# A streaming encoder step on one core: 32-row products of the mixer grouped, three costs of its schedule set anew, last sums of squares moved in between the products

## The chip, the cores and the metric

The kernel runs on one core of one Trainium2 chip. The time is the device time of one execution in microseconds (us). Before the change three runs took 2301.47, 2303.37 and 2303.8 us; the median is 2303.37 us. One more execution was recorded by the hardware profiler; it took 2301.52 us, and from its first to its last instruction 2299.8 us.

The engines are called by short names in the profile: PE is TensorE's products, PEld its weight loads, DVE is VectorE, ACT ScalarE, POOL GpSimd, SP the queue that starts DMAs. One float32 product of the program stands in the trace as two records with a weight load each; one product of split operands stands as one record.

## The reference, cut to what matters

A batch of 544 rows (512 of a prompt, 32 of a running sample) of width 1024 passes two layers. The first has a Mamba-2 mixer, the second attention; each has two feed-forward blocks and a gated input embedding, and a final norm ends the step. The two places that the change touches are the mixer's scan and the end.

```python
def ssd_scan(xdt, a, Bm, Cm, s0, chunk_len):
    ...
        y_diag = jnp.einsum('bijg,bijge,bjgep->bigep', cb, decay, x_c)      # inside a chunk: 32 heads in 4 groups of 8
        y_off = jnp.einsum('bign,bgepn->bigep', C_c, state) * jnp.exp(a_cs)[..., None]
        ...
        return new_state, y_diag + y_off
...
        gate = jax.nn.sigmoid(rms_norm(x, ple_norm[i]) @ ple_w_gate[i])
        x = x + gate * (p[i] @ ple_w_proj[i])
    return rms_norm(x, final_norm), ...
```

The prompt is scanned in four chunks of 128 rows, the sample is a fifth chunk of 32 rows with its own carried state. The final norm needs, for each row, the sum of squares over all 1024 values of x.

## The kernel before, in words

Activations lie transposed: eight tiles `x[c]` of 128 features by 544 rows, the rows in two halves of 272. Dense weights are split into a high and a low part (`whi`, `wlo`), and a 128-by-128 block of a dense product is three matmuls for each half of 272 columns (`product`, line 284).

**The mixer** (`mamba`, line 972) runs as generators under a planner (`Plan`, line 65). Each step of a generator names an engine and a cost in us ("T" is TensorE); `Plan.run` (line 139) keeps a modelled time for each engine, always takes the step that could begin first, and writes its instructions. The engines execute in just the order so written (`ordered`), so the costs decide the order of instructions and nothing else. The dense products (`dense`, ranked last) come in the order `MSEQ = "i0 z0 i1 i2 z1 o0 i3 z2 o1 z3 o2 o3"`: inputs, gates and outputs of the four groups. Between them the planner puts the scan. For group g and chunk c, `turn_x` and `turn_b` transpose, `decay` makes `ex` (inside the chunk) and `ab` (decay times C, a POOL product), `state` makes the next `st`, and `output` (line 1318) makes y: for each of the eight heads one product with `ex` and, from chunk 1 on, one with the old state. `emit(t)` (line 1336) writes two heads h = 2t and 2t+1: head by head, first the product of `xd` and `ex` (as many rows as the chunk has), then that of `st` and `ab` (128 rows). The even head goes to partitions 0 to 63 of the result, the odd head to 64 to 127. Four such steps are written per chunk (line 1343); the planner is told 0.44 us each for chunk 0, 0.87 for chunks 1 to 3, 1.2 for the sample. In the sample chunk the first product has 32 rows and the second 128, both move 32 columns.

**The end** (`ple`, line 944, called for layer 1 at line 2050) is not under the planner: its engines' order is made by the compiler's own list scheduling. It goes through `order` (line 1995): features m = 0 to 3 with both halves, 4 to 7 with the first half, then 7, 6, 5, 4 with the second. For each, `product` into a bank `pg`, then on DVE `ft` (times the norm), on ACT a sigmoid, on DVE `fu` and the new `x`, and then `last` (line 2022), which squares x (`sq`, in the second half `sq1`), scales x on POOL, and hands the squares on. The sums of squares are TensorE products with a matrix of ones: `add_square` (line 1997) for the second half, one tile at a time, and `finish(0)` (line 2004) for the first half, both called by `last`. `finish(a)` then makes the inverse root (`ry`, `rm`, `rfin`), the outputs `out` and their DMAs. In the order of the code, `finish(0)` stands straight after the products of (7, second half), and an `add_square` after those of (6), (5) and (4); `finish(1)` writes the last one.

All instructions written through the wrapper at line 192 show as L193 in the profile; the tile names tell them apart.

Of the kernel before, what the change touches and what calls it, by code (L numbers as in the profile page):

```python
# [10 lines left out]
P = 128  # L11
D = 1024
KC = D // P
TP = 512
TS = 32
T = TP + TS
# [28 lines left out]
NZB, NY, NYH = 1, 2, 4  # L45

RGNORM, RSCAN, RCONV, RGATE, ROUT, RSTEP = 39, 4, 20, 45, 2, 41

FIRST = [0, 1, 2, 3], [0, 1, 2, 3], [0, 1, 2, 3], [0, 1, 2, 3]
GROUPS = [(4, 5), (6, 7)], [(8, 9), (10, 11)], [(12, 13), (14, 15)], [(16, 17), (18, 19), (20, 21)]  # L50
# [130 lines left out]
def _body(tc, io):  # L181
# [17 lines left out]
    V, S, G, TE = (Engine(n, e) for n, e in (("V", nc.vector), ("S", nc.scalar), ("G", nc.gpsimd), ("T", nc.tensor)))  # L199
# [4 lines left out]
    with ExitStack() as ctx:  # L204
# [66 lines left out]
        def weight_parts(pool=pool):  # L271
            return [pool.tile([P, 1024], F32R, tag=t, name=t, bufs=2) for t in ("whi", "wlo")]
# [668 lines left out]
            split(ph, pl, pr)  # L941
            return [(ph[:, k, :], pl[:, k, :]) for k in range(2)]

        def ple(i, norm, after, psum, tmp, ring, order, keep=lambda m: None):
            ps_in = ple_inputs(i, tmp)
            prj = tmp.tile([P, KC, T], F32, tag="plp", name="plp")
            for m in range(KC):
                if m % 4 == 0:
                    wp = load_w(io["wple"][i, m // 4], 1024)
                pp = psum()  # L950
                product(pp, wp, ps_in, off=(m % 4) * 256)
                S.activation(halves(prj[:, m, :]), pp[:, :, :H], AF.Copy)
            r, held = None, {}
            for m, which in order:
                def cut(v):
                    return v[:, which[0] * H:(which[-1] + 1) * H].rearrange("p (a b) -> p a b", a=len(which))
                if m not in held:
                    held[m] = load_w(io["wpg"][i, m], 1024, parts=keep(m))
                pg = psum()
                product(pg, held[m], norm.parts, which=which)  # L960
                if r is None:
                    r = norm.scale(psum, ring)
                t = tmp.tile([P, T], F32, tag="ft", name="ft", bufs=2)
                V.tensor_tensor(out=cut(t), in0=pg[:, which[0]:which[-1] + 1, :H], in1=cut(r), op=ALU.mult)
                S.activation(cut(t), cut(t), AF.Sigmoid)
                u = tmp.tile([P, T], F32, tag="fu", name="fu", bufs=2)
                V.tensor_tensor(out=cut(u), in0=cut(t), in1=cut(prj[:, m, :]), op=ALU.mult)
                V.tensor_tensor(out=cut(x[m]), in0=cut(x[m]), in1=cut(u), op=ALU.add)
                after(m, which, t)


        def mamba(norm, after, ready, ahead):
            with tc.tile_pool(name="mt", bufs=1, reuse_waits="tile") as tmp, \
# [16 lines left out]
                got = {}  # L990
# [327 lines left out]
                def output(g, c):  # L1318
                    off, n = chunks[c]
                    src = off if c < 4 else SOFF  # L1320
                    xs = got["x", g]
                    need = [("ex", g, c), ("xd", g, c), ("xw", g, c), ("cd", g, c)]
                    yield "wait", *need
                    if c > 0:
                        yield "wait", ("st", g, before(c))
                    if c == 0:
                        yield "get", "y"
                        got["y", g] = tmp.tile([P, 4, T], F32, tag="y", name="y", bufs=NY)
                        yield "set", ("y0", g)
                    else:  # L1330
                        yield "wait", ("y0", g)
                    yield "get", "aux"
                    py = aux()
                    xd, ex, ab = got["xd", g, c], got["ex", g, c], got["ab", g, c]

                    def emit(t):
                        for b in range(2):
                            h = 2 * t + b
                            dst = py[64 * b:64 * b + 64, t * P:t * P + n]
                            TE.matmul(dst, xd[:n, h, :], ex[:n, h, :], start=True, stop=c == 0)  # L1340
                            if c > 0:
                                TE.matmul(dst, got["st", g, before(c)][:, h, :], ab[:, h, :], start=False, stop=True)
                    for t in range(4):
                        yield "T", (1.2 if n < P else 0.87) if c else 0.44, lambda: emit(t)
                    yield "set", ("y", g, c)
                    yield "put", "ex"
                    yield "put", "xd"
                    yield "put", "ab"
                    pyv = py[:, :].rearrange("p (t i) -> p t i", t=4)[:, :, :n]
                    yv = got["y", g][:, :, off:off + n]  # L1350

                    def skip(t):
                        V.scalar_tensor_tensor(out=yv[:, t], in0=xs[:, t, src:src + n], scalar=dskip[:, 4 * g + t:4 * g + t + 1], in1=pyv[:, t],
                                               op0=ALU.mult, op1=ALU.add)
                    for t in range(4):
                        yield "W", v_cost(n) + 0.06, lambda: skip(t)
                    yield "put", "aux"
                    yield "set", ("out", g, c)
# [638 lines left out]
        def add_square(last=False):  # L1997

            if not total:
                total.append(psum())  # L2000
                TE.matmul(total[0][:, 1, :H], ones, acc[:, H:], start=True, stop=False, skip_group_check=True)
            TE.matmul(total[0][:, 1, :H], ones, waiting.pop(0), start=False, stop=last, skip_group_check=True)

        def finish(a):
            cols = slice(a * H, a * H + H)
            if a:
                add_square(last=True)
                at_once(rsqrt_ops(total[0], [], D, "rfin", (a,), rfin))
            else:
                at_once(rsqrt_ops(psum(), [acc, squares[a]], D, "rfin", (a,), rfin))  # L2010
            for c in range(0, KC, 2):
                o = end.tile([P, 2, H], F32, tag="out", name="out", bufs=4)
                for b in range(2):
                    if (c + b, a) in scaled:
                        e = G if a == 0 or c + b in (1, 3) else V
                        e.tensor_tensor(out=o[:, b, :], in0=x[c + b][:, cols], in1=rfin[:, cols], op=ALU.mult)
                    else:
                        V.scalar_tensor_tensor(out=o[:, b, :], in0=x[c + b][:, cols], scalar=gains[:, NORMS["fin"], c + b:c + b + 1],
                                               in1=rfin[:, cols], op0=ALU.mult, op1=ALU.mult)
                nc.sync.dma_start(io["y"][:, c:c + 2, cols], o)  # L2020

        def last(c, which, t):
            cols = slice(which[0] * H, (which[-1] + 1) * H)
            ending = (c, which) in ((7, (0,)), (4, (1,)))
            if which == (1,):
                sq = end.tile([P, H], F32, tag="sq1", name="sq1", bufs=4)
                if waiting:
                    add_square()
                waiting.append(sq)
                if ending:  # L2030
                    V.tensor_tensor(out=sq, in0=x[c][:, cols], in1=x[c][:, cols], op=ALU.mult)
                    S.activation(table, t[:, H:H + 1], AF.Abs_reciprocal_sqrt)
                else:
                    S.activation(sq, x[c][:, cols], AF.Square)
                    G.tensor_scalar(x[c][:, cols], x[c][:, cols], gains[:, NORMS["fin"], c:c + 1], 0.0, op0=ALU.mult, op1=ALU.add)
                    scaled.add((c, 1))
                if c == 7:
                    finish(0)
                return
            sq = acc if c == 0 else pool.tile([P, T], F32, tag="sq", name="sq", bufs=2)  # L2040
            if ending:
                V.tensor_tensor(out=sq[:, cols], in0=x[c][:, cols], in1=x[c][:, cols], op=ALU.mult)
                squares[0] = sq
            else:
                S.activation(sq[:, cols], x[c][:, cols], AF.Square)
                if c:
                    G.tensor_tensor(out=acc[:, cols], in0=acc[:, cols], in1=sq[:, cols], op=ALU.add)
                G.tensor_scalar(x[c][:, cols], x[c][:, cols], gains[:, NORMS["fin"], c:c + 1], 0.0, op0=ALU.mult, op1=ALU.add)
                scaled.update((c, a) for a in which)
        ple(1, np1, last, psum, tmp, few, order, lambda m: weight_parts(end) if m in (4, 5) else None)  # L2050
        finish(1)
        xg["st"].close()
        later["st"].close()
# [78 lines left out]
```

## Time and profile before

| | us |
|---|---|
| median of three runs | 2303.37 |
| profiled execution | 2301.52 |
| its span, first to last instruction | 2299.8 |
| PE busy in the span | 2267.0 (99%) |
| DVE / ACT / POOL busy | 1680.0 / 1011.1 / 575.7 |
| mixer with its approaches, 384 to 830 us: PE busy of 446 | 441.83 |
| last 38 us, 2262 to 2300: PE busy | 24.75 |

A busy time of PE is modelled from pipelined matmuls, so a busy PE is not yet one at its peak; how many records of one shape go through in a stretch says more. A row of the timeline gives the start, the length from the first record's start to the last one's end, and the number of records; the distance between two rows' starts is what a group of records costs. "granted" clock is the share of TensorE's 2.4 GHz that the chip allowed in a stretch: 1.00 is 2.4 GHz and 0.50 is 1.2 GHz.

### The profile page before, as it was taken

Reading aid. Unit: us, or ns where it says so; the run is one execution under the profiler, and the core shown is the slowest. Engines: PE = TensorE matmul, PEld = TensorE weight load, DVE = VectorE, ACT = ScalarE, POOL = GpSimd, SP = SyncE. Lnnn points to the kernel's source line nnn. Section 1 sums busy time; section 2 is a strip of 40 time slices with the busy share of each in tenths; the row PEclk is TensorE's granted clock in tenths of the full one; section 3 lists DMA queues with packets and bytes.
Section 4 is the critical chain, followed back from the end, with each engine's and each line's share of the span. In section 5 each row is a group of like instructions: output and inputs, shape, how many; then the busy total and the mean of one; then the engine's idle time right before and its main releaser. Section 6 shows DMA issues by size and latency. Waiting matters only on the chain.

```text
span 2299.8 us, 42811 instructions
## 1 busy us (share of the span) xinstructions
PE 2267.0 (99%) x17937; PEld 2207.0 (96%) x17937; DVE 1680.0 (73%) x2201; ACT 1011.1 (44%) x1489; POOL 575.7 (25%) x541
## 2 busy tenths in 40 slices
PE   9999999999999999999999999999998999999997
PEld 9999999989899999999999999999985899999997
DVE  7777786679777676777757767778678576777857
ACT  5333334567646353333345533333468353333343
POOL 1221122244324122121221122121234122221224
PEclk9999999999999999999999999999999999999999
DMA  5233323333433232333232423332311132333232
GB/s 170 85 91 106 97 67 90 112 100 94 110 97 99 75 119 79 106 93 106 65 99 91 130 81 104 100 98 65 89 45 56 47 117 86 92 106 97 67 100 76
DMA packets 111537, 213.19 MB, mean 93 GB/s; under 512 B 12400, under 2 KB 33520, under 8 KB 111344
## 3 DMA queue, kind: packets, MB, share of 16 engines
q1 hardware_dynamic: 108464, 204.92, 29.7%
q10 hardware_dynamic: 2880, 5.53, 0.7%
q8 instruction: 141, 2.31, 0.4%
q14 instruction: 52, 0.43, 0.1%
HBM read 204.83 MB, written 5.60 MB: 91 GB/s over the span
## 4 chain that ended last, share of the span: by engine, by line
PE 92%; DVE 4%; ACT 2%; issue 1%; POOL 1%; DMA 1%; SPq 0%; DVEq 0%; ACTq 0%; POOLq 0%
PE mm L193 82%; PE z L193 3%; PE aux L193 3%; PE o L193 1%; PE f L193 1%; PE tr L193 1%; DVE wlo L193 1%; ACT whi L193 1%; DVE xl L193 1%; POOL ab L193 0%; DVE x L193 0%; DVE e L193 0%; DMA wraw<-in_wpg 0%; DVE fu L193 0%; DVE rm L193 0%
## 5 line engine op out<-in xcount | busy, mean ns | idle before, releaser
L193 PE MATMUL mm<-xh,whi 128*128 128x272 f32 x2096 | 513.0, 293 | 2.3 <-DVE x L193 1.0
L193 PE MATMUL mm<-xh,wlo 128*128 128x272 f32 x2096 | 506.2, 289 | 1.8 <-DVE wlo L193 1.8
L193 PE MATMUL mm<-xl,whi 128*128 128x272 f32 x2096 | 507.7, 290 | 0.3 <-DVE xl L193 0.3
L193 PEld LDWEIGHTS mm<-xh,whi 128*128 128x128 f32 x2096 | 358.6, 189 | 10.5 <-issue 7.2
L193 PEld LDWEIGHTS mm<-xh,wlo 128*128 128x128 f32 x2096 | 358.3, 189 | 2.3 <-DVE wlo L193 2.2
L193 PEld LDWEIGHTS mm<-xl,whi 128*128 128x128 f32 x2096 | 358.3, 190 | 0.7 <-DVE xl L193 0.7
L193 ACT ACTIVATE whi<-wraw 128x1024 fp32r<-128x1024 f32 (+3 forms) x215 | 184.2, 858 | 374.5 <-PE mm L193 263.3
L193 PE MATMUL mm<-xfh,whi 128*128 128x272 f32 x1152 | 332.4, 289 | 0.0
L193 PE MATMUL mm<-xfl,whi 128*128 128x272 f32 x1152 | 332.3, 288 | 0.0
L193 PE MATMUL mm<-xfh,wlo 128*128 128x272 f32 x1152 | 332.2, 288 | 0.0
L193 DVE TENSOR_TENSOR wlo<-wraw,whi 128x1024 fp32r<-128x1024 f32 (+3 forms) x252 | 257.0, 1020 | 72.6 <-ACT whi L193 54.6
L193 PE MATMUL mm<-hh,whi 128*128 128x272 f32 x1408 | 291.5, 288 | 0.0
L193 PE MATMUL mm<-hh,wlo 128*128 128x272 f32 x1408 | 291.1, 288 | 0.0
L193 PE MATMUL mm<-hl,whi 128*128 128x272 f32 x1408 | 290.9, 288 | 0.0
L193 ACT ACTIVATE whi<-a 128x1024 fp32r<-128x1024 f32 x127 | 134.9, 1062 | 319.8 <-PE mm L193 214.4
L193 DVE TENSOR_TENSOR wlo<-a,whi 128x1024 fp32r<-128x1024 f32 x145 | 178.4, 1230 | 101.7 <-ACT whi L193 67.2
L193 PEld LDWEIGHTS mm<-hl,whi 128*128 128x128 f32 x1408 | 221.5, 189 | 0.0
L193 PEld LDWEIGHTS mm<-hh,whi 128*128 128x128 f32 x1408 | 221.2, 188 | 0.0
L193 PEld LDWEIGHTS mm<-hh,wlo 128*128 128x128 f32 x1408 | 220.7, 189 | 0.0
L193 PEld LDWEIGHTS mm<-xfh,wlo 128*128 128x128 f32 x1152 | 217.1, 188 | 0.0
L193 PEld LDWEIGHTS mm<-xfl,whi 128*128 128x128 f32 x1152 | 217.1, 188 | 0.0
L193 PEld LDWEIGHTS mm<-xfh,whi 128*128 128x128 f32 x1152 | 217.1, 188 | 0.0
(290 smaller groups left out, 4108.0 us busy)
## 6 DMA issues: line engine op xcount, KB each, us to landing
a<-in_wgu SPq DMA_DIRECT2D x145, 512.0 KB, 3.9
wraw<-in_wd SPq DMA_DIRECT2D x128, 256.0 KB, 2.7
wraw<-in_win SPq DMA_DIRECT2D x41, 512.0 KB, 3.6
wraw<-in_wgu SPq DMA_DIRECT2D x29, 512.0 KB, 3.7
wraw<-in_wd SPq DMA_DIRECT2D x32, 384.0 KB, 3.1
ab<-acs_d SPq DMA_DIRECT2D x16, 512.0 KB, 4.7
wraw<-in_wout SPq DMA_DIRECT2D x16, 512.0 KB, 3.6
wraw<-in_wpg SPq DMA_DIRECT2D x16, 512.0 KB, 3.6
```

What stands on the lines that cost most here:

```text
L193: ins = getattr(self.engine, op)(*args, **kw)
```

## The change

It has three parts. In the mixer, the sample chunk's sixteen products are written as one step: first all eight with 32 rows, then all eight with 128 rows, the even and odd head still in turn; the planner is told 1.8 us for all. For the other chunks the cost of a step is 0.24 (chunk 0) and 0.46 (chunks 1 to 3). In the end, `ple` writes its product feature block by feature block and calls `between` after four of the eight; through it, `finish(0)` comes amid the products of (6, second half), and one `add_square` each amid those of (5) and (4); `finish(1)` writes the last two. In layer 0 `ple` gets no `between`, and its instructions stay the same.

```diff
+TSSD = 0.24, 0.46
...
-                product(pg, held[m], norm.parts, which=which)
+                for c in range(KC):
+                    if c == KC // 2 and between:
+                        between(m, which)
+                    product(pg, held[m], norm.parts, only=c, which=which)
...
-                    for t in range(4):
-                        yield "T", (1.2 if n < P else 0.87) if c else 0.44, lambda: emit(t)
+                    def emit_sample():
+
+                        for old in range(2):
+                            for h in range(8):
+                                t, b = divmod(h, 2)
+                                dst = py[64 * b:64 * b + 64, t * P:t * P + n]
+                                if old:
+                                    TE.matmul(dst, got["st", g, before(c)][:, h, :], ab[:, h, :], start=False, stop=True, skip_group_check=True)
+                                else:
+                                    TE.matmul(dst, xd[:n, h, :], ex[:n, h, :], start=t == 0, stop=False, skip_group_check=True)
+                    if n < P:
+                        yield "T", 1.8, emit_sample
+                    else:
+                        for t in range(4):
+                            yield "T", TSSD[c > 0], lambda: emit(t)
...
             if a:
+                add_square()
                 add_square(last=True)
...
-                if waiting:
-                    add_square()
...
-                if c == 7:
-                    finish(0)
...
+        def between(m, which):
+
+            if which == (1,) and m == 6:
+                finish(0)
+            elif which == (1,) and m < 6:
+                add_square()
```

## Rows read from the trace of the kernel before

**Rows 1.** The page: busy time and share of the span (part 1), and the chain of work that ended last, by engine (part 4).

```profile
PE 2267.0 (99%) x17937; PEld 2207.0 (96%) x17937; DVE 1680.0 (73%) x2201; ACT 1011.1 (44%) x1489; POOL 575.7 (25%) x541
...
PE 92%; DVE 4%; ACT 2%; issue 1%; POOL 1%; DMA 1%; SPq 0%; DVEq 0%; ACTq 0%; POOLq 0%
```

**Rows 2.** Who PE waited for between 384 and 830 us (the mixer with its approaches): us in total, times, longest.

```profile
PE aux L193 <- POOL ab L193: 1.2, 2, 0.9
PE aux L193 <- POOL xw L193: 0.9, 1, 0.9
PE aux L193 <- DVE btok L193: 0.8, 1, 0.8
PE mm L193 <- DVE wlo L193: 0.7, 1, 0.7
```

**Rows 3.** The timeline of PE around the sample chunk of groups 0, 1, 2 and 3: start, us from the first record's start to the last one's end, operation, shape, records. The sample's products are `aux<-ex,xd` (32 rows) and `aux<-ab,st` (128 rows); the last row of each stretch is the work after them.

```profile
487.78 0.30 PE L193 MATMUL aux<-ex,xd 32*64 32x32 f32 x2
488.94 0.30 PE L193 MATMUL aux<-ab,st 128*64 128x32 f32 x2 [0.86 <-POOL ab L193]
...
492.38 0.82 PE L193 MATMUL mm<-xh,whi 128*128 128x272 f32 x2
...
580.17 0.30 PE L193 MATMUL aux<-ex,xd 32*64 32x32 f32 x2
580.40 0.30 PE L193 MATMUL aux<-ab,st 128*64 128x32 f32 x2
...
583.84 1.40 PE L193 MATMUL aux<-xw,btok 128*128 128x512 f32 x2
...
633.44 0.30 PE L193 MATMUL aux<-ex,xd 32*64 32x32 f32 x2
...
637.10 0.52 PE L193 MATMUL mm<-yh,whi 128*128 128x272 f32 x2
...
741.26 0.30 PE L193 MATMUL aux<-ex,xd 32*64 32x32 f32 x2
741.85 0.30 PE L193 MATMUL aux<-ab,st 128*64 128x32 f32 x2 [0.29 <-POOL ab L193]
...
745.44 0.82 PE L193 MATMUL mm<-xh,whi 128*128 128x272 f32 x2
```

**Rows 4.** PE's groups by shape between 430 and 826 us: busy us, mean ns of one record.

```profile
L193 PE MATMUL aux<-ex,xd 32*64 32x32 f32 x64 | 9.5, 228 | 0.0
```

**Rows 5.** The timeline of PE where products of 64 weight columns stand in a run: a chunk of 128 rows with both kinds of product (482 us), chunk 0 of group 2, which has the products with `ex` alone (588 us), and, in the attention, four records of 32 rows ahead of records of 128 rows (1766 us).

```profile
482.08 0.45 PE L193 MATMUL aux<-ex,xd 128*64 128x128 f32 x4
482.35 0.40 PE L193 MATMUL aux<-ab,st 128*64 128x128 f32 x4
482.57 0.44 PE L193 MATMUL aux<-ex,xd 128*64 128x128 f32 x4
...
588.55 1.09 PE L193 MATMUL aux<-ex,xd 128*64 128x128 f32 x16
589.58 0.49 PE L193 MATMUL aux<-C,B 128*128 128x128 f32 x2
...
1766.03 0.43 PE L193 MATMUL o<-an,vt 32*64 32x128 f32 x4
1766.39 0.33 PE L193 MATMUL o<-sa,vc 128*64 128x128 f32 x2
```

**Rows 6.** Stretches of 3.4 us that follow the sample chunks of groups 0, 1, 2 and 3: us, PE busy (records), granted clock, DMA share, GB/s.

```profile
492.40:495.80 3.40, 3.40 (x16) 0.50 0.59 159
...
584.56:587.97 3.41, 3.41 (x15) 0.50 0.58 154
...
637.10:640.50 3.40, 3.40 (x29) 1.00 0.51 153
...
745.00:748.40 3.40, 3.40 (x17) 0.50 0.21 77
```

**Rows 7.** A stretch of the scan of group 1: us, then busy time (and instructions) of PE, PEld, DVE, ACT and POOL, granted clock, DMA share, GB/s.

```profile
520.00:555.00 35.00, 35.00 (x280) 33.70 (x279) 31.40 (x57) 24.56 (x43) 13.40 (x20) 1.00 0.29 93
```

**Rows 8.** The timeline of PE in the last 30 us: the sums of squares (products with ones).

```profile
2273.57 0.62 PE L193 MATMUL mm<-acc,ones 128*128 128x272 f32 x2
2274.95 0.73 PE L193 MATMUL mm<-sq,ones 128*128 128x272 f32 x2 [0.77 <-DVE sq L193]
...
2283.58 0.73 PE L193 MATMUL mm<-sq,ones 128*128 128x272 f32 x2 [0.97 <-ACT sq L193]
...
2287.15 0.62 PE L193 MATMUL mm<-sq,ones 128*128 128x272 f32 x2
2289.79 0.73 PE L193 MATMUL mm<-sq,ones 128*128 128x272 f32 x2 [2.02 <-DVE sq L193]
```

**Rows 9.** The timelines of DVE, ACT and POOL in the same stretch.

```profile
2274.46 0.44 DVE L193 TENSOR_TENSOR sq<-x 128x272 f32<-128x272 f32 x1
...
2281.43 0.71 DVE L193 TENSOR_TENSOR fu<-ft,plp 128x272 f32<-128x272 f32 x1 [0.95 <-ACT ft L193]
...
2288.34 0.44 DVE L193 TENSOR_TENSOR fu<-ft,plp 128x272 f32<-128x272 f32 x1 [0.56 <-ACT ft L193]
...
2279.67 1.28 ACT L193 ACT_TABLE_LOAD   x1 [1.78 <-DVE ft L193]
...
2286.25 0.95 POOL L193 TENSOR_SCALAR x<-x,gains 128x272 f32<-128x272 f32 x2
```

More of the change, by code (lines that the diff above doesn't have):

```diff
@@ L942, in ple_inputs, with ple @@
             return [(ph[:, k, :], pl[:, k, :]) for k in range(2)]
-        def ple(i, norm, after, psum, tmp, ring, order, keep=lambda m: None):
+        def ple(i, norm, after, psum, tmp, ring, order, keep=lambda m: None, between=None):
             ps_in = ple_inputs(i, tmp)
@@ L2049, in last @@
                 scaled.update((c, a) for a in which)
-        ple(1, np1, last, psum, tmp, few, order, lambda m: weight_parts(end) if m in (4, 5) else None)
+        def between(m, which):
[3 more added lines that the diff above has]
+                add_square()
+        ple(1, np1, last, psum, tmp, few, order, lambda m: weight_parts(end) if m in (4, 5) else None, between)
         finish(1)
```

## The prediction

> **What bounds the kernel now.** I read the page first: PE is busy for 99% of the span and takes 92% of the chain that ended last [rows 1]. So a change is worth what it takes from PE's own queue, or from the places where PE stands still. A busy PE need not do much, though, so in the mixer I looked at the waits and then at single stretches of the timeline. Between 384 and 830 us PE stands still for only 446 - 441.83 = 4.2 us, and the largest entries are waits of 0.7 to 1.2 us for single products of POOL and DVE [rows 2]. The mixer is bound by the order and the pace of PE's records, and nothing else hides what is saved there. DVE comes next: 31.4 of 35 us in the densest stretch of the scan [rows 7], which leaves it below PE everywhere.
>
> The reader should see three things. First, the sample chunk, the smallest of five, takes PE longest. Its sixteen products last 4.60, 3.67, 3.66 and 4.18 us in groups 0 to 3 (from the first row to the work after them [rows 3]), 16.1 us together; a chunk of 128 rows does the same sixteen, with four times the columns, at 0.22 us for four records [rows 5], so 32 records in 1.76 us. Second, right after three of these four blocks the granted clock is 0.50 for 3.4 us, that is 1.2 instead of 2.4 GHz, and 15 to 17 records go through instead of 29 [rows 6]. Third, in the last 30 us PE waits 0.77 us for a square from DVE and 0.97 us for one from ACT [rows 8].
>
> **The sample's products.** Two records of a pair span 0.30 us and one lasts about 0.22 to 0.23 [rows 3, 4], so the second starts some 0.08 after the first. The next pair starts 0.23 after the first, 0.15 after the second. That 0.15 is paid at each change between 32 and 128 rows; where 128 rows follow 128 rows it isn't seen, though heads alternate there as well [rows 5]. The attention has the same: four records of 32 rows span 0.43 at about 0.27 each, so the last starts at 0.16, and the first of 128 rows comes at 0.36, 0.20 later [rows 5]. Those four records also show that two halves of 64 output columns run side by side, at 32 rows too: four starts fit in 0.16.
>
> New block, if the halves run side by side: in each run of eight products a half has four products of two records, eight records at 0.08, so the last starts at 0.56, and 0.15 passes until the next kind: 0.71 a run, 1.42 for two. Four blocks take 5.7 us instead of 16.1, which saves 10.4. In group 0 the `ab` product of POOL is there only at 488.94 [rows 3]; the first run would be over at 487.78 + 0.71 = 488.49, so 0.45 remains a wait. In group 3 it is there at 741.85, before 741.26 + 0.71. Net **10.0 us**.
>
> The new shape, 32 rows in a run of sixteen records, isn't in the trace, so bounds: with the pace of 16 records in 1.03 us that chunk 0 has at four times the columns [rows 5], 32 records and two changes take 2.06 + 0.30 = 2.4 us, which saves 6.6. With one half after the other, 32 records at 0.08 and two changes take 2.7 us or a little more, which saves 5.3. Better than 1.42 by at most 0.3 a block (1.2 in all), if a record's start could come sooner than 0.08 after the last on its half. I take 1.42, since the row nearest in shape, the sample's own pair, has the 0.08, and the row nearest in rows has the halves side by side.
>
> The Trainium skill has a rule that speaks against the grouping: "TensorE: Matmul & The Clock Gate", the mechanism in its part on packing small matmuls, says that a weight load overlaps with running matmuls only where its row group differs. By it the old order would be the overlapped one. The row shows the contrary: 0.15 at each change of rows, 0.08 without. "TensorEngine Tiling (Array Packing)", key properties, has a change of tiling mode drain the engine, and there the trace agrees.
>
> **The clock.** Each fall costs the 29 - 16 = 13 records that didn't pass, 3.40 x 13/29 = 1.5 us. PE came out of 3.6 us of 32-column records in all three cases; group 2's block, just as long, was followed by full clock [rows 6], so it isn't certain even then. A block of 1.4 us is less than half as long; I take it that none falls: 3 x 1.5 = **4.6 us**. Bounds: 0 and 4.6.
>
> **The order.** The model's TensorE time in one group's outputs falls from 4 x 0.44 + 12 x 0.87 + 4 x 1.2 = 17.0 to 4 x 0.24 + 12 x 0.46 + 1.8 = 8.3 us, 35 us in four groups. The engine measured 0.26 (16 records in 1.03 us, four steps) and 0.44 (eight records at 0.22 per four) [rows 5], so these are near the truth and the old ones near twice it. It adds no instruction. The planner has room for more dense products between two steps of the scan, so scan products stand later in PE's queue relative to dense ones, and their inputs are the more likely there; in return POOL's and DVE's work, which the model prices as before, is packed denser against PE's time. A wrong place costs all queued behind it on PE, dense products included: the waits known from before are 0.8 to 0.9 us [rows 2]. Bounds: -2 (those for `xw`, `btok` and the rest vanish) and +18 (each of 20 chunks waits 0.9). I take **+0.5**: the old order was twice wrong in its cost and still left 4.2 us of waiting in 446.
>
> **The end.** PE's records are the same, so the gain is in the two waits. `finish(0)` now follows 12 products of (6) at 0.125 (29 in 3.4 us is 0.117, so 1.4 to 1.5 us): it comes at 2273.57 + 1.5 = 2275.1, and DVE's square is done at 2274.46 + 0.44 = 2274.90 [rows 8, 9]. The wait of 0.77 is gone. What is late next is the sum of (6)'s square, which before came 0.97 after PE was free. The chain to it (`ft`, table load, sigmoid, `fu`, `x`, square) starts when (6) is done, 0.77 earlier, but the root's table load waits for sums that are about 0.6 later; so I put the square at 2282.5 to 2282.9, and PE asks for it amid (4), at about 2283.0. Both waits go: 1.74. Against that, the last `fu` and `x` run while POOL still scales (until 2287.2), and `fu` beside POOL took 0.71 instead of 0.44 [rows 9]: 0.4 lost on the path that ends the kernel. Net **1.3 us**. Bounds: 1.74, and -1.3 if the compiler's list scheduling puts one more table load (1.28 [rows 9]) on that path. The outputs' DMAs come as before, eight on SP, four of them up to half a us later, behind nothing but themselves; the last four come 1.3 earlier. In layer 0 the split product is the same sequence, at nothing.
>
> **Sum.** 10.0 + 4.6 - 0.5 + 1.3 = 15.4 us; 2301.5 - 15.4 = 2286.1, on the profiled execution, which is 1.9 below the median of the three runs. One more fall of the clock (1.5 us) would explain most of that distance, and such a fall would go as well, so I predict **2287**.
>
> **Rivals.**
> (a) The halves don't run side by side at 32 columns, or runs of equal rows lose an overlap of weight loads: 2.7 us a block, 5.3 saved instead of 10.0, 2291. For it: the sample's records have shown no second half running yet. Against it: the attention's four records. The rule of "TensorE: Matmul & The Clock Gate" named above comes to this time too.
> (b) The new order costs 5 to 13 us of waits on PE (each of 20 chunks waiting 0.25 to 0.65 us for `ab`, `ex` or `xw`): 2291 to 2299. For it: DVE at 90% in a stretch of the scan [rows 7]; against it: the old order's small waits.
> (c) Slower: the same mechanism further on. In the new order PE stands before `aux<-ab,st` until POOL has written `ab`, in each chunk of all four groups. From 0.77 us per chunk (15.4/20) the gain is gone, and at 1.0, a little over the longest wait there is now [rows 2], the kernel takes 2301.5 + 4.6 = 2306.
> (d) The clock still falls after the blocks, as a low pace is left in them: 2291.
> (e) The change doesn't do what it says: the 0.23 per product belongs to 32 columns and not to the change of rows, the blocks stay as long and the clock falls as before; only the end gains: 2300 to 2302.
>
> **Chances.** Forecast 0.60 (2282 to 2291 by its own bounds), a 0.10, b 0.13, c 0.05, d 0.06, e 0.06. About 0.2% (4.6 us) is what a measurement of this kernel can tell from no change. Against the median, faster is below 2298.8: the forecast, a, d and most of b, 0.87; the same is e and the end of b, 0.08; slower is c, 0.05. The range from 2281 to 2296 leaves out c, e and the upper part of b, and a little at the lower end.
>
> **What would show it.** Sample blocks of 1.4 to 1.8 us with two groups of rows, 32 rows first; granted clock 1.00 between 440 and 830 us; no more than about 5 us of waits on PE in the mixer; no wait before the sums at the end, and the last sum at about 2288 less what the mixer gave, 1.3 earlier against the products. Blocks of 2.7 us speak for a, many waits for `ab` or `ex` for b or c, clock falls in spite of short blocks for d. I am wrong if PE's idle time in the mixer grows by over 5 us or if the blocks stay above 3 us.

## The result and the profile after

| | before | after |
|---|---|---|
| median, us | 2303.59 (2301.47 to 2306.64, 4 runs) | 2287.18 (2283.51 to 2288.59, 4 runs) |
| profiled execution, us | 2301.52 | 2283.51 |
| its span, us | 2299.8 | 2281.8 |

The ratio is 0.9917, interval 0.9905 to 0.9929: 16.4 us between the medians, 18.0 between the two profiled executions. The forecast was 2287. One run of an experiment below (`e2_costs`) took 3133.44 us at a mean granted clock of 0.652 and is left out of its ratio.

The page, parts 1 and 4, as [rows 1]:

```profile
PE 2252.0 (99%) x17937; PEld 2195.6 (96%) x17937; DVE 1676.6 (73%) x2201; ACT 1014.1 (44%) x1491; POOL 567.7 (25%) x540
...
PE 93%; DVE 4%; ACT 2%; issue 1%; DMA 1%; POOL 0%; DVEq 0%; SPq 0%; ACTq 0%; POOLq 0%
```

The same 17937 matmuls, PE at 99% as before: 15.0 us of busy time are gone although no record is. A page alone would not show why; the timeline of PE at the four sample chunks does (last row of each stretch: the work after them, as in [rows 3]):

```profile
500.46 0.65 PE L195 MATMUL aux<-ex,xd 32*64 32x32 f32 x16
501.05 0.66 PE L195 MATMUL aux<-ab,st 128*64 128x32 f32 x16
501.64 0.52 PE L195 MATMUL mm<-xh,whi 128*128 128x272 f32 x2
...
576.85 0.65 PE L195 MATMUL aux<-ex,xd 32*64 32x32 f32 x16
...
578.02 0.52 PE L195 MATMUL mm<-xh,whi 128*128 128x272 f32 x2
...
635.16 0.65 PE L195 MATMUL aux<-ex,xd 32*64 32x32 f32 x16
...
636.33 0.52 PE L195 MATMUL mm<-xh,whi 128*128 128x272 f32 x2
...
728.83 0.65 PE L195 MATMUL aux<-ex,xd 32*64 32x32 f32 x16
...
730.00 0.51 PE L195 MATMUL mm<-xh,whi 128*128 128x272 f32 x2
```

Each block takes 1.17 to 1.18 us; together 4.7 instead of 16.1, so 11.4 us. The stretches that follow them in groups 0, 1 and 3, where the clock fell before, as [rows 6], and the one stretch at a granted clock of 0.50 between the kernel's first and last 10 us, in the attention (us, PE busy with records, granted clock, DMA share, GB/s):

```profile
501.64:505.04 3.40, 3.40 (x31) 1.00 0.56 174
578.02:581.42 3.40, 3.40 (x32) 1.00 0.49 144
...
730.00:733.40 3.40, 3.40 (x31) 1.00 0.46 84
...
1726.96:1733.79 6.83, 6.83 (x31) 0.50 0.00 0
```

31 or 32 records at 2.4 GHz where 15 to 17 went through at 1.2 GHz: none of the three falls in the mixer is left. Who PE waited for between 384 and 825 us, as [rows 2]:

```profile
PE mm L195 <- DVE yl L195: 1.1, 1, 1.1
PE mm L195 <- DVE wlo L195: 0.7, 1, 0.7
PE mm L195 <- DVE cu L195: 0.3, 1, 0.3
```

2.1 us instead of 4.1, and other waits than before: scan products wait for nothing now, and the two new entries stand before dense products. The 0.7 for `wlo` is in both and belongs to the product behind the mixer (at 809.33, before at 826.09). The last product of the mixer's outputs (`mm<-yh,wlo`) starts at 802.44 instead of 819.20, 16.8 us earlier, although the same records ahead of the mixer stand 0.2 later (386.22 instead of 386.03); the mixer itself gained 17.0. Of that 11.4 are the blocks, 4.6 three falls of the clock at the forecast's 1.5, and 1.0 is left for the order; the waits outside the sample blocks fell by 0.8 (4.1 less the 1.2 for `ab` inside the blocks is 2.9, now 2.1).

The rest is the end. The sums of squares on PE, as [rows 8]:

```profile
2258.12 0.62 PE L195 MATMUL mm<-acc,ones 128*128 128x272 f32 x2
...
2269.33 0.73 PE L195 MATMUL mm<-sq,ones 128*128 128x272 f32 x2 [1.25 <-ACT sq L195]
...
2271.80 0.72 PE L195 MATMUL mm<-sq,ones 128*128 128x272 f32 x2 [1.75 <-DVE sq L195]
```

The waits of 0.77 and 0.97 are gone and the sums between the rows shown wait for nothing, but the sum for feature 5 now waits 1.25, where before it waited for nothing (2287.15 in [rows 8]). From the end of the products of feature 7, second half, to the last sum it was 2289.79 - 2273.57 = 16.2 us; now the first sum stands behind 12 products of feature 6 (1.5 us), so it is 2271.80 - 2258.12 + 1.5 = 15.2. The end gained 1.0 us. What is late now shows on DVE and POOL:

```profile
2264.09 6.06 POOL L195 TENSOR_TENSOR out<-x,rfin 128x272 f32<-128x272 f32 x7 [3.20 <-DVE rfin L195]
...
2265.21 1.01 DVE L195 SCALAR_TENSOR_TENSOR out<-x,gains,rfin 128x272 f32<-128x272 f32 x1
...
2267.92 0.88 DVE L195 TENSOR_TENSOR x<-x,fu 128x272 f32<-128x272 f32 x1
2268.73 0.43 DVE L195 TENSOR_TENSOR ft<-mm,r 128x272 f32<-128x272 f32 x1
...
2269.72 0.73 DVE L195 TENSOR_TENSOR fu<-ft,plp 128x272 f32<-128x272 f32 x1 [0.56 <-ACT ft L195]
...
2270.48 0.61 DVE L195 TENSOR_TENSOR x<-x,fu 128x272 f32<-128x272 f32 x1
...
2271.13 0.62 DVE L195 TENSOR_TENSOR sq<-x 128x272 f32<-128x272 f32 x1
```

PE was through with feature 4 at 2269.33 - 1.25 = 2268.08, but DVE took up its `ft` only at 2268.73, behind `x` of feature 5; and `fu`, `x` and the square take 0.73, 0.61 and 0.62. In the kernel before, the same chain (PE's last product for feature 4, then DVE; `fu` and a square of 0.44 are in [rows 9]):

```profile
2287.02 0.29 PE L193 MATMUL mm<-nh,wlo 128*128 128x272 f32 x1
2287.35 0.44 DVE L193 TENSOR_TENSOR ft<-mm,r 128x272 f32<-128x272 f32 x1 [1.71 <-PE mm L193]
...
2288.82 0.44 DVE L193 TENSOR_TENSOR x<-x,fu 128x272 f32<-128x272 f32 x1
```

There `ft` started 0.04 after PE (2287.02 + 0.29 = 2287.31), and each step of the chain took 0.44.

### The profile page after: what moved, and what is told of

Its sections match the earlier page's. It is cut to its first block, busy times and chain, and to the rows that moved or that the text cites. A ratio compares the mean times of both kernels' runs of the same rounds, so it can differ in the third digit from the quotient of the medians.

```text
span 2281.8 us, 42795 instructions
## 1 busy us (share of the span) xinstructions
PE 2252.0 (99%) x17937; PEld 2195.6 (96%) x17937; DVE 1676.6 (73%) x2201; ACT 1014.1 (44%) x1491; POOL 567.7 (25%) x540
## 4 chain that ended last, share of the span: by engine, by line
PE 93%; DVE 4%; ACT 2%; issue 1%; DMA 1%; POOL 0%; DVEq 0%; SPq 0%; ACTq 0%; POOLq 0%
PE mm L195 83%; PE z L195 3%; PE aux L195 3%; PE o L195 1%; PE f L195 1%; PE tr L195 1%; DVE wlo L195 1%; ACT whi L195 1%; DVE xl L195 1%; DVE x L195 1%; DVE e L195 0%; DVE fu L195 0%; DMA wraw<-in_wpg 0%; DMA x<-in_x 0%; DVE rm L195 0%
```

## The experiments

The theory after this result: the time in the sample blocks is paid per change between 32 and 128 rows; the clock fell because of the long, slow blocks; the two new durations matter because they put scan products behind the dense work that their inputs need; and DVE's queue took over the end. Rivals: the columns' halves, and not the changes of rows, set the blocks' pace; the clock or the order gained by chance of position; the wait at the end came from the mixer's new order or from POOL's work.

| kernel | median, us | ratio to before, interval | gain of the mixer, us |
|---|---|---|---|
| grouping alone (`e1_group`) | 2292.61 | 0.9947, 0.9932 to 0.9962 | 10.2 |
| durations alone (`e2_costs`) | 2301.95 | 0.9982, 0.9973 to 0.9991 | 1.4 |
| end alone (`e3_end`) | 2307.77, one run | | -5.3 |
| even heads first (`e4_halves`) | 2283.99, one run | | 15.3 |
| pairs of heads (`e5_pairs`) | 2285.30, one run | | 14.5 |
| feature 7 scaled by POOL (`e6_pool7`) | 2283.18 | 0.9907, 0.9894 to 0.9920 | 17.0 |
| two old durations (`e7_oldt`) | 2289.12 | 0.9940, 0.9924 to 0.9955 | 12.9 |
| the changed kernel again (`after_again`) | 2288.46 | 0.9923, 0.9911 to 0.9936 | 17.0 |

The kernel before had a median of 2306.43 us beside e1, e2, e4 and e5, and 2305.14 beside the others. The last column is from the one profiled execution of each: how much sooner than in the kernel before the last `mm<-yh,wlo` comes, counted from the record that starts there at 386.03 us. What comes ahead of the mixer is not in it; falls of the clock inside the mixer are.

**Grouping alone.** In the kernel before, with `emit_sample` as in the change, the old durations and the old end:

```diff
-                    for t in range(4):
-                        yield "T", (1.2 if n < P else 0.87) if c else 0.44, lambda: emit(t)
...
+                    if n < P:
+                        yield "T", 4.8, emit_sample
+                    else:
+                        for t in range(4):
+                            yield "T", 0.87 if c else 0.44, lambda: emit(t)
```

> The kernel before with the sample's sixteen products grouped by rows and nothing else: the planner still counts 4.8 us for them and the old costs for the other chunks, the end is as before. Theory 1 (the time went with the changes between 32 and 128 rows and with the clock falls behind them): blocks of 1.2 us in groups 1 to 3 and some 1.8 in group 0, where the product of ab is late; no granted clock of 0.50 between 440 and 830 us; 10.8 + 4.6 = 15 us less than the kernel before, 2288 to 2289. Theory 2 (the gain came from the new order of the mixer's instructions): blocks short as well, but waits take their place, and the time is above 2297.

0.9947, which is 12.2 us of 2303.6, between what the two theories had said. Three blocks are as short as in the changed kernel or nearly so (487.83 to 489.59 with a wait of 0.52 for `ab`, 630.15 to 631.32, 735.45 to 736.64); the fourth is followed by a wait of 0.43 for `xw` (575.86 to 577.53). But a new wait has come, and right after it the clock falls (timeline of PE, then the stretch with its granted clock):

```profile
583.40 1.18 PE L193 MATMUL aux<-ex,xd 128*64 128x128 f32 x16 [2.70 <-DVE y L193]
```

```profile
584.28:587.69 3.41, 3.30 (x10) 0.50 0.54 159
```

PE's waits between 384 and 825 us are 6.6 us in all, against 4.1 before and 2.1 in the changed kernel, and the mixer ends 6.6 us later than there (809.07 against 802.44); 1.5 of that is the fall of the clock. The grouping alone made PE too early for the order that the old durations had written.

**Durations alone.** The kernel before with alternating products, told at 1.8 for the sample and 0.24 and 0.46 for the rest:

```diff
-                    for t in range(4):
-                        yield "T", (1.2 if n < P else 0.87) if c else 0.44, lambda: emit(t)
+                    def emit_sample():
+
+                        for t in range(4):
+                            emit(t)
+                    if n < P:
+                        yield "T", 1.8, emit_sample
+                    else:
+                        for t in range(4):
+                            yield "T", (0.24, 0.46)[c > 0], lambda: emit(t)
```

> The kernel before with the three new costs of the schedule and nothing else: the sample's sixteen products alternate between 32 and 128 rows as before, in one step of 1.8 us, and the end is as before. Theory 1: blocks of 3.7 us, granted clock of 0.50 behind most of them, some 1 us fewer waits in the mixer: 2300 to 2304, no difference that can be measured. Theory 2: most of the gain is here, 2290 to 2294.

0.9982, 4.1 us, at the edge of what can be told from none. The waits of PE between 384 and 825 us fall to 1.0 us (0.3 for `cu` beside the row below); the 0.7 for `wlo`, at 826.45 here, lies outside, so against the 4.1 before it is 1.7. Three blocks stay at 3.67 us (502.02 to 505.69 in group 0); that of group 1 takes 4.23 (582.41 to 586.64), as the clock falls within it. The clock falls behind or within three of them, one fall of double length (PE's waits between 384 and 825 us, then the stretches with their granted clock):

```profile
PE mm L193 <- DVE yl L193: 0.7, 1, 0.7
```

```profile
506.50:509.91 3.41, 3.41 (x17) 0.50 0.56 154
585.01:591.84 6.83, 6.83 (x33) 0.50 0.53 156
649.86:653.27 3.41, 3.41 (x17) 0.50 0.52 154
```

That is one stretch of 3.4 us more than before, and one more comes at 8.15 us, ahead of the mixer. The records ahead of the mixer stand 1.75 us later than in the kernel before, and the mixer ends only 0.35 later, in spite of the 1.5 that the one stretch more inside it costs: at equal clock the order gave some 2.9 us, of which the waits explain 2.4 (4.1 to 1.7). The order has no cost of its own. The clock falls at long blocks in another order, too, though not at the same ones (groups 0, 1 and 2 here, 0, 1 and 3 before): it goes with the blocks and not with their places.

**Even heads first.** In the changed kernel, which keeps the two changes of rows:

```diff
-                            for h in range(8):
+                            for h in (0, 2, 4, 6, 1, 3, 5, 7):
```

> The changed kernel, but in each run of rows first the four even heads and then the four odd ones, so that the two halves of 64 output columns no longer take turns. The instructions and the order of all else are the same. If the short block needs both halves side by side: records at 0.058 us one after the other, 16 x 0.058 + 0.15 = 1.1 a run, 2.2 us a block, 1.0 more in each of four, and perhaps granted clock of 0.50 behind some. If turns between halves don't matter: 1.2 us a block as in the changed kernel.

The block of group 0 in its timeline of PE:

```profile
499.87 0.91 PE L195 MATMUL aux<-ex,xd 32*64 32x32 f32 x16
500.71 0.91 PE L195 MATMUL aux<-ab,st 128*64 128x32 f32 x16
501.55 0.52 PE L195 MATMUL mm<-xh,whi 128*128 128x272 f32 x2
```

A run takes 0.84 us instead of 0.59. Strictly one half after the other would be 1.03: a run is 0.44 for the eight records of a half and 0.15 for the change, so 2 x 0.44 + 0.15. Taken one by one, the starts form two rows, each with 0.058 between records; the second begins 6 ns after the fifth of the eight records of the first. So the other half does not wait until the first is through. This leaves a part of the rival: halves in turn are worth 0.5 us of a block, of 2.5 that the block lost; the changes of rows are the larger part. Over the whole mixer 1.6 us are lost against the changed kernel: 4 x 0.5, less 0.4 by which a wait for `yl` is shorter.

**Pairs of heads.** In the changed kernel, two heads with `ex`, the same two with `ab`, and so on: eight runs instead of two.

```diff
-                        for old in range(2):
-                            for h in range(8):
+                        for h0 in range(0, 8, 2):
+                            for old in range(2):
+                                for h in (h0, h0 + 1):
...
```

> The changed kernel, but the sample's products go by pairs of heads: two with 32 rows, two with 128 rows, four times; 7 changes of rows within a block instead of 1 (15 in the kernel before). If each change costs 0.15 us: two records per half at 0.08, then 0.15, 0.23 for each of eight pairs, 1.8 us a block, 0.65 more than the changed kernel in each of four groups, no clock falls. If the number of records and not the changes sets the length: 1.2 us.

The same block here:

```profile
500.49 0.30 PE L195 MATMUL aux<-ex,xd 32*64 32x32 f32 x4
500.72 0.31 PE L195 MATMUL aux<-ab,st 128*64 128x32 f32 x4
...
502.37 0.52 PE L195 MATMUL mm<-xh,whi 128*128 128x272 f32 x2
```

The step of 0.23 to 0.24 us is the same for four records in two halves as it was for two in one [rows 3]: what is paid is the change. Fifteen, seven and one change in a block take 3.66, 1.88 and 1.17 us, so (1.88 - 1.17)/6 = 0.12 for each of six changes. (The step from fifteen to seven sets the halves side by side as well and says less on the changes alone.) Over the whole mixer 2.5 us are lost against the changed kernel: 4 x 0.71, less 0.4 of the wait for `yl`. With 1.88 us, as with e4's 1.68, the clock stays at 1.00 from 440 to 825 us.

**End alone.** The kernel before with the change's third part only:

```diff
-                product(pg, held[m], norm.parts, which=which)
+                for c in range(KC):
+                    if c == KC // 2 and between:
+                        between(m, which)
+                    product(pg, held[m], norm.parts, only=c, which=which)
...
+            if which == (1,) and m == 6:
+                finish(0)
+            elif which == (1,) and m < 6:
+                add_square()
```

> The kernel before with the change's end alone: sums of squares in the middle of the later products, the mixer as before. If the end brings what the traces of before and after suggest, the stretch from the end of the products of the second half's last chunk but the closing one (chunk 7) to the last sum of squares shrinks from 16.2 us to about 15.2 us, and the whole run by 1.0 us, which one time can't show. The forecast's own step said 1.3 us. The sums behind them on TensorE should start without a wait, except the one for chunk 5, which waits 1.2 to 1.3 us for a square, since VectorE's chain of temporaries ends last there. Rival: the wait came from the mixer's other order or from the run's own clock, then it is absent here and the stretch shrinks by 1.7 us.

The sums of squares in its timeline of PE:

```profile
2281.78 0.62 PE L194 MATMUL mm<-acc,ones 128*128 128x272 f32 x2
...
2293.05 0.73 PE L194 MATMUL mm<-sq,ones 128*128 128x272 f32 x2 [1.29 <-ACT sq L194]
...
2295.51 1.27 PE L194 MATMUL mm<-sq,ones 128*128 128x272 f32 x2 [1.74 <-DVE sq L194]
```

2295.51 - 2281.78 + 1.5 = 15.2 us against 16.2: 1.0 gained, and the wait of 1.29 is there without the mixer's new order. The rival falls. The time of this run, 2307.77, says nothing on 1 us: its clock was low for 6.8 us three times, from within the sample blocks of groups 0, 2 and 3 on (492.28, 639.05 and 748.27), twice as long as in the profiled execution of before. With the same mixer it lost 5.3 us there.

**Feature 7 scaled by POOL.** In the changed kernel, so that DVE's output of 1.01 us ahead of `ft` of feature 5 goes to POOL:

```diff
                 if ending:
                     ...
+                    G.tensor_scalar(x[c][:, cols], x[c][:, cols], gains[:, NORMS["fin"], c:c + 1], 0.0, op0=ALU.mult, op1=ALU.add)
+                    scaled.add((c, 0))
```

> The changed kernel, with the gains of the first half of chunk 7 multiplied on GpSimd, as for the other chunks, so that VectorE no longer makes that chunk's output in one operation of 1.01 us ahead of the temporaries of chunk 5; the output goes to GpSimd, too. If VectorE's own queue sets the wait of 1.25 us before chunk 5's sum, the temporaries of chunk 5 start 0.8 to 1.0 us earlier, that wait falls to 0.3 us or less, and the last sum comes 0.5 to 0.9 us earlier against chunk 7's products; the time falls by as much, near the limit of what can be told. If VectorE is slowed by GpSimd's work beside it, or ScalarE's temporaries end last, the wait stays over 0.9 us. Rival: GpSimd's longer row of outputs ends later than the last sum's own chain, then the end stays where it is or moves out by up to 1 us.

The sums of squares in its timeline of PE, then its timelines of POOL and DVE:

```profile
2257.20 0.62 PE L195 MATMUL mm<-acc,ones 128*128 128x272 f32 x2
...
2267.68 0.72 PE L195 MATMUL mm<-sq,ones 128*128 128x272 f32 x2 [0.35 <-ACT sq L195]
...
2270.69 0.72 PE L195 MATMUL mm<-sq,ones 128*128 128x272 f32 x2 [2.28 <-DVE sq L195]
```

```profile
2263.39 6.94 POOL L195 TENSOR_TENSOR out<-x,rfin 128x272 f32<-128x272 f32 x8 [3.20 <-DVE rfin L195]
...
2267.37 0.44 DVE L195 TENSOR_TENSOR ft<-mm,r 128x272 f32<-128x272 f32 x1 [0.20 <-PE mm L195]
2268.36 0.44 DVE L195 TENSOR_TENSOR fu<-ft,plp 128x272 f32<-128x272 f32 x1 [0.56 <-ACT ft L195]
2268.84 0.88 DVE L195 TENSOR_TENSOR x<-x,fu 128x272 f32<-128x272 f32 x1
2269.75 0.88 DVE L195 TENSOR_TENSOR sq<-x 128x272 f32<-128x272 f32 x1
```

The wait for feature 5 falls from 1.25 to 0.35, so DVE's queue had set it. But from the first sum to the last it is 13.5 us against 13.7: 0.2 gained, not 0.5 to 0.9. The wait itself was no price: the sum of feature 5 waited beside the chain of feature 4, which ends last. Of that chain the edit took 0.61: `ft` starts at 2267.37, 0.04 after PE (2267.68 - 0.35 = 2267.33) instead of 0.65; and `fu` is 0.29 shorter. Against that, `x` and the square, beside POOL's eighth output, take 0.88 each instead of 0.61 and 0.62, 0.53 more, and PE is through with feature 4 later by 0.17 against the first sum. The sum is 0.20 of gain, as measured. The ratio's interval overlaps that of the changed kernel beside it, so no better version is established here.

**Two old durations.** The changed kernel with its grouping, its 1.8 for the sample, and its end:

```diff
-TSSD = 0.24, 0.46
+TSSD = 0.44, 0.87
```

> The changed kernel with the two durations of the schedule's model as they were (0.44 and 0.87 instead of 0.24 and 0.46), the sample's products in one run and the end as changed. If the two durations carry what the order brings, the waits of TensorE in the mixer rise from 2.1 us to 4 to 6.6 us, and the time is 2 to 4 us above the changed kernel's. If the sample block's own duration (1.8 here, 4.8 in the kernel with the grouping alone) carries it, the waits stay at 2 to 3 us and the time is within 1 us of the changed kernel's.

Who PE waited for between 384 and 825 us:

```profile
PE aux L195 <- DVE y L195: 1.5, 1, 1.5
PE aux L195 <- DVE xd L195: 1.2, 1, 1.2
```

The waits are 5.9 us with 0.8 for `ex` and those for `xw`, `ab` and `wlo`, and the mixer ends at 808.16 instead of 802.44. The records ahead of the mixer stand 1.7 us later than in the changed kernel, behind a fall of the clock at 8.2 us, and no fall is in the mixer; so the order explains 4.0 of these 5.7, and the waits 3.8 of the 4.0. The whole time shows less of it: 0.9940 against 0.9923 is 3.9 us, with intervals that overlap, and the medians are 0.7 apart, as the clock in the attention differs from run to run (next paragraph). It is the two durations of the other chunks, and not the sample's own, that keep PE from arriving ahead of its inputs.

**The changed kernel again**, without an edit.

> The changed kernel once more, beside the others on the same chip: 2284 to 2288.5 us, ratio to the kernel before 0.991 to 0.993. A clock of 0.50 for 3.4 us or more comes in none of the places behind the sample blocks; one in the attention stage may come or not, and accounts for 1.7 or 3.4 us of what runs differ by.

2288.46, ratio 0.9923. Its profiled execution, 2288.73, is 5.2 us above the first one (2283.51). The blocks and the waits in the mixer are the same within 0.01 us, the end within 0.03; the stretches at half clock in the attention are not (columns as above):

```profile
1718.90:1722.31 3.41, 3.23 (x13) 0.50 0.00 0
1729.14:1732.55 3.41, 3.41 (x18) 0.50 0.00 0
1739.38:1742.79 3.41, 3.41 (x16) 0.50 0.07 20
1811.06:1814.47 3.41, 3.41 (x17) 0.50 0.48 148
```

Four such stretches and one at 8.8 us, against two in a row (6.8 us): three more at 1.5 are 4.6 of the 5.2 us. The mean granted clock points the same way in the other runs, which have no trace: 0.994 in the two at 2288.2 and 2288.9, as in the profiled one, and 0.996 in the one at 2284.6. So between the two profiled executions these stretches are most of the difference, and most likely of this kernel's scatter in all.

## Why the prediction was right, step by step

**The bound.** Right: PE's own records were what the mixer waited for; all that was taken from them came out at the end of the mixer (17.0 us, the same in the three profiled executions with this mixer) and went through to the span (18.0).

**The blocks, 10.0, measured 11.4.** The mechanism was right (0.15 at each change of rows, halves side by side); the term was mis-sized. Records in a run of equal rows soon follow each other at 0.058 us on a half and not at the 0.08 that a single pair shows, and both halves start 7 ns apart: 0.59 us a run instead of 0.71, 1.17 a block instead of 1.42, which makes 1.0 over four blocks. The other 0.45 is the wait for `ab` in group 0, which the forecast kept: with all of the change the block stands 13 us later (500.46 instead of 487.78), and `ab` is there. With the grouping alone the forecast's 0.45 did come, as 0.52. The first rival is refuted by the dose of changes: fewer changes of rows were faster at each step (3.66, 1.88, 1.17 us). The prediction had also put a rule behind that rival, and read it too widely. In the Trainium skill, "TensorE: Matmul & The Clock Gate", the mechanism in its part on packing small matmuls, the weight load that is pulled ahead is one that "targets a non-conflicting `row_grp` (or the background weight buffer)". A product of 32 rows shares its rows with one of 128 (32*64 and 128*64 in [rows 3]), so their row groups conflict and did not make the old order the overlapped one; the runs agree, with 0.12 to 0.15 us lost at each change.

**The clock, 4.6.** Right: no fall in the mixer of the changed kernel, in either profiled execution, nor in those with blocks of 1.68 and 1.88 us; falls behind or within nine of the twelve blocks of 3.66 us in before, e2 and e3, whatever the order. The single fall in e1 came behind a wait of 2.7 us. With blocks of 1.17 us and 2.4 GHz behind them, the rivals d and e are refuted. The 1.5 for each holds by the pace, too: pairs of dense records follow each other after 0.25 us at 2.4 GHz and 0.45 at 1.2 (e2, at 592 and 588 us), so 3.41 us at 1.2 GHz cost 3.41 x 0.20/0.45 = 1.5. In most runs the falls may have cost more: the kernel before had medians 3.6 and 4.9 us above its profiled execution beside the experiments, at mean granted clocks of 0.991 to 0.994 (0.994 there), and e3's falls were twice as long; no trace shows where the others lay. That a shorter block removes the fall is shown; why the chip lowers the clock where it does is not, and in e3 it fell 1.5 us after the start of group 3's block, so the length of the block alone does not decide it.

**The order, -0.5, measured +1.0.** The one step with the wrong sign: "the old order was twice wrong in its cost and still left 4.2 us of waiting" was no argument, since the old order's places fitted the old, long blocks. The bound below, a gain of 2, was passed when taken alone (2.9 in e2). And the terms were not independent: with short blocks and the old durations the waits rise to 5.9 or 6.6 us, so within this change the measured durations are worth 4 to 5 us, most of which only keeps what the grouping gave. The rivals b and c, waits for `ab`, `ex` or `xw` in the new order, are refuted; such waits come in the old one (`ex`, `xd`, `y` in e7).

**The end, 1.3, measured 1.0.** Both waits went as said, and PE was through with feature 4 even 2.3 us earlier against feature 7 (11.5 us instead of 13.7), more than the two waits of 1.74: each stop had also cost some 0.26 behind the wait. (From the first sum to the product behind the sums it was 2275.32 - 2273.57 = 1.75, now 2258.84 - 2258.12 = 0.72, and the wait was 0.77 of the 1.03.) Mis-sized was what follows: from there to the last sum it is 3.7 us instead of 2.5 (2289.79 - 2287.31). `ft` starts 0.65 after PE instead of 0.04, behind `x` of feature 5, and `fu`, `x` and the square take 1.96 instead of 1.32; so 1.2 where the forecast put 0.4. For `fu` and `x` beside POOL its 0.4 was about right (1.34 instead of 0.88); what it had left out is DVE's queue, which the earlier products fill (0.61), and the square (0.18). e3 shows that this belongs to the end alone, e6 that both parts of it, queue and POOL, are on the path. No further table load came on the path.

**The sum.** 11.4 + 4.6 + 1.0 + 1.0 = 18.0, as between the profiled executions. The forecast's 15.4 was short by 2.6 there (2286.1 for 2283.5). That the median came within 0.2 us of 2287 is luck: it lies 3.7 above this kernel's own profiled execution, the shortest of its four, and the same kernel's next four runs had a median of 2288.46. The parts taken alone give 12.2 (e1) + 4.1 (e2) + 1.0 (e3, from the trace) = 17.3, but they don't add up for that: in the traces the mixer gains 10.2 and 1.4 with one part and 17.0 with both.

## What to carry to other kernels

Where small products of unlike row counts alternate, look at the distance between the starts of their records and compare it with a run of one kind: the change may cost more than the product, and a reordering within the block adds no record. When one step of a hand-made schedule becomes faster, the durations in its model have to follow, or the saved time comes back as waits in the same stretch. At the end of a kernel, list the second-latest chain before pricing a wait that goes: here DVE's queue and POOL's work beside it gave back half of what PE saved (1.2 of 2.3 us).

## What the runs showed of the hardware

- Records of 32 columns in a run of equal rows follow at 0.058 us on each half of the output columns, the two halves 7 ns apart: 16 products, 32 records and one change of rows in 1.17 us. With the halves one after the other in the program (e4), a run takes 0.84 and not the 1.03 of one half strictly after the other: records of the second half start before the first is through.
- A PE that the profile shows as busy can lose its clock: group 1's block of 3.66 us in the kernel before has no wait, and 1.2 GHz follows for 3.4 us. In before, e2 and e3 the clock fell behind or within nine of twelve such blocks, for 3.4 or 6.8 us; right behind the 28 blocks with fewer changes of rows (1.17 to 1.88 us) it fell at none.
- DVE's `x` and square on 128x272 took 0.44 us with POOL idle, 0.61 beside POOL's scaling by gains, and 0.88 to 0.90 beside its outputs (products of two tiles). `fu` is less regular: 0.44 in one case beside the outputs, 0.73 to 0.76 in others.
